# A two-layer decoder trunk: the first attention's beginning in written order, products issued ahead, contexts split as they end, and three smaller edits

## The chip, the cores and the metric

The kernel runs on one core of a Trainium2 chip. The metric is the device time of one execution in microseconds; the time before is the median of three runs. TensorE (PE) multiplies, VectorE (DVE), ScalarE (ACT) and GpSimd (POOL) work on tiles, and SyncE (SP) issues most transfers.

## The reference, cut to what matters

x is 512 tokens of 1024 features. Layer 0 mixes tokens with 16 heads of 64 whose scores carry a forgetting bias; layer 1 uses another attention that the change does not touch, apart from the order of its output projection.

```python
h = rms_norm(x, norm_mix_g[0])
proj = h @ fox_w_in[0]                      # q, k, v (1024 columns each) and 16 gate columns
cum = cumsum(log_sigmoid(gate + fox_b_f[0]), axis=tokens)
s = q @ k.T * 64**-0.5 + cum[query] - cum[key]      # causal
ctx = softmax(s) @ v
x = x + ctx @ fox_w_out[0]
x = x + square(relu(rms_norm(x, norm_ffn_g[0]) @ w_up)) @ w_down
...                                          # layer 1: latent attention, the same MLP
return rms_norm(x, final_norm_g)
```

## The kernel before, in words

Activations stand as tiles of 128 features by 512 tokens, so x is eight tiles and a linear layer is a sum over eight blocks of weights. Every number is split into a high part, rounded to the type that TensorE takes (ACT casts), and a low part, the rest (DVE subtracts). A product of two split numbers is three products: high by high, high by low, low by high (`three`, lines 260 to 269). One of 512 columns is what the texts call a product.

The root mean square is applied late: products are made of x times the gain, and the factor 1/rms of each token is multiplied into what comes out. It is computed from the sum of squares by token (`token_sums`, line 297, products with a column of ones), by three Newton steps (`rsqrt_of`, line 314, on GpSimd unless `alone`, then on DVE), and spread along a row by products with the identity (`along_tokens`, line 333; `rstd_tile`, line 341, copies it out).

Weights come in pieces of up to 128 x 1024, in the order of `pieces()` (line 74). `piece()` (line 250) hands out the next one and emits the load, cast and subtraction of it and of the one after. Two raw buffers and three of each part turn round (`raw`, `whi`, `wlo`).

The program is written as a sequence of tile operations. A scheduler then orders each engine's instructions by its own estimate of when operands are ready; where `order["on"]` names engines, their instructions stay in written order. Before the change this holds only in the MLPs and in the beginning of the second attention.

**The beginning (lines 470 to 559).** Eight x tiles, a gate piece of 128 columns and the first q and k pieces are loaded on SP's queue. Each x tile is scaled and split. Then PE makes the gate logits (24 products, the 16 gate columns padded to 128), q of the first head pair (24), the token sums, k (24) and the row of 1/rms. Then come four pieces of value weights, 24 products each, into four PSUM banks; after the first of these DVE finishes q and k (`qk_parts`) and the gate's running sum in nine doubling steps (`forget_sums`, line 522), which is stored to DRAM (`csc`) and loaded again, spread over partitions, as the bias tile `nb` of each pair (`start`, line 577).

**The attention (lines 415 to 449, 575 to 646).** A pair of heads takes four steps, of 512, 384, 256 and 128 keys. A step makes scores in two banks (`scores`), reduces, exponentiates and scales them on DVE and ACT (`soft_step`), and three steps later turns them by transposes (`turn_unit`). After a pair's last turn, `values` makes its context. Between steps a `Filler` issues products of coming work: 12 per step and 18 in the middle of a pair's end, `FILL1`, and 12 ahead of the first scores (line 643). Its work is, in order, q and k of pairs 1 to 7 (48 each), two groups of value columns (96 each) and parts of the output projection (`out_begin`, line 451) for three blocks and later two more. A part waits for its context (`ready`), and each context is split when the projection first asks for it (`ctx_part`, line 634). The other blocks of the projection follow in `out_proj` (line 648).

**The MLP (`ffn`, line 669)** runs by a list of due steps. In layer 0 `row` (line 756) makes the row of 1/rms; it is first used for the last eight blocks of hidden features (`up_post`, line 759).

**The end (`finish`, line 1299; `by_tokens`, line 1317).** The last eight output blocks of 128 tokens by 512 columns take 24 products each. After each the block is added to x, squared and summed, 1/rms is found by three Newton steps of two instructions, and two halves are scaled and stored.

## Time and profile before

| | us |
|---|---|
| median of three runs | 1130.95 (1130.09 to 1131.11) |
| the profiled execution | 1130.42 |
| its span, first to last instruction | 1128.6 |
| PE busy | 1113.4 |
| DVE busy | 781.4 |
| ACT busy | 581.3 |

The page gives busy time by engine and the chain that ended last. The timeline lists instructions in order of their start, repeated ones merged (xN); in square brackets stands how long the engine was idle before and what it waited for. A product's duration there includes its way through the array, so that products overlap: what one costs is read from the distance between starts. Nearly all operations are recorded through line 112, so tiles and stretches tell them apart: `acc`, `sc`, `tp`, `go`, `up`, `keep` are PSUM banks, `whi` and `wlo` parts of weights, `r` split activations, `t` temporaries.

### The profile page before, as it was taken

The numbers are of one execution on the slowest core, as the hardware profiler recorded it, in microseconds if no ns is written. First come the engines' busy times: TensorE is split into PE (matmuls) and PEld (weight loads), VectorE is DVE, ScalarE is ACT, GpSimd is POOL, SyncE is SP. The second block draws the span as 40 slices with busy tenths as digits, with TensorE's granted clock in tenths as the row PEclk, the third lists the DMA queues.
The fourth block names the chain that finished last, engine by engine and source line by source line (L and its number), as shares of the span: only waits on it lengthen the run. The fifth ranks groups of instructions, "written<-read, shape, count | busy, mean of one in ns | idle before, by whom it ended". The sixth has DMA issues, their size and how long they took to land.

```text
span 1128.6 us, 14263 instructions
## 1 busy us (share of the span) xinstructions
PE 1113.4 (99%) x5340; PEld 912.0 (81%) x5340; DVE 781.4 (69%) x1420; ACT 581.3 (52%) x1060; POOL 19.5 (2%) x71
## 2 busy tenths in 40 slices
PE   8999999999999999999999999999999999999997
PEld 6778887788888888888888877888888888888885
DVE  6797788764566667577895878738265765765784
ACT  5565665644555454434454767635465544444622
POOL 1000000001000000000001000000100000000000
PEclk9999999999999999999999999999999999999999
DMA  5422222143724415311344212213442611611402
GB/s 190 132 81 102 80 74 77 57 139 104 265 109 135 126 38 167 106 63 38 112 146 130 83 44 75 94 56 109 162 159 75 186 58 57 198 58 43 132 1 76
DMA packets 36822, 116.66 MB, mean 103 GB/s; under 512 B 4224, under 2 KB 4864, under 8 KB 36752
## 3 DMA queue, kind: packets, MB, share of 16 engines
q1 hardware_dynamic: 35888, 114.15, 31.1%
q10 hardware_dynamic: 864, 1.60, 0.4%
q8 instruction: 42, 0.69, 0.3%
q14 instruction: 28, 0.23, 0.1%
HBM read 109.40 MB, written 6.32 MB: 103 GB/s over the span
## 4 chain that ended last, share of the span: by engine, by line
PE 95%; DVE 2%; ACT 1%; DMA 1%; issue 0%; SPq 0%; ACTq 0%
PE up L112 35%; PE acc L112 20%; PE go L112 19%; PE sc L112 8%; PE tp L112 8%; PE keep L112 6%; DVE t L112 1%; ACT t L112 1%; DVE r L112 1%; DMA nb<-csc 0%; DMA t<-xT 0%; DVE wlo L112 0%; ACT whi L112 0%; ACT r L112 0%; DVE rs L112 0%
## 5 line engine op out<-in xcount | busy, mean ns | idle before, releaser
L112 PE MATMUL acc<-r,whi 128*128 128x512 f32 x606 | 196.4, 404 | 5.2 <-ACT whi L112 4.9
L112 PE MATMUL up<-r,r 128*128 128x512 f32 x808 | 192.7, 391 | 0.0
L112 PEld LDWEIGHTS up<-r,r 128*128 128x128 f32 x808 | 151.3, 188 | 31.4
L112 PE MATMUL up<-r,whi 128*128 128x512 f32 x544 | 170.9, 391 | 0.0
L112 DVE TENSOR_TENSOR wlo<-raw,whi 128x1024 fp32r<-128x1024 f32 (+3 forms) x95 | 111.4, 1173 | 48.3 <-ACT whi L112 37.6
L112 DVE TENSOR_TENSOR t<-s,t 128x512 fp32r<-128x512 f32 x84 | 58.0, 690 | 121.8 <-ACT t L112 121.7
L112 PEld LDWEIGHTS acc<-r,whi 128*128 128x128 f32 x606 | 111.1, 190 | 30.0 <-ACT whi L112 4.9
L112 ACT ACTIVATE s<-up 128x512 f32<-128x512 f32 x56 | 33.4, 597 | 190.0 <-PE up L112 190.0
L112 ACT CAST whi<-raw 128x1024 fp32r<-128x1024 f32 (+3 forms) x95 | 95.4, 1007 | 69.1 <-PE acc L112 30.6
L112 PE MATMUL acc<-r,wlo 128*128 128x512 f32 x303 | 119.7, 395 | 0.0
L112 PEld LDWEIGHTS up<-r,whi 128*128 128x128 f32 x544 | 101.8, 188 | 20.9
L112 PE MATMUL up<-r,wlo 128*128 128x512 f32 x288 | 112.3, 390 | 0.0
L112 PE MATMUL go<-r,t 128*128 128x512 f32 x360 | 86.5, 389 | 0.0
L112 PE MATMUL sc<-r,r 128*128 128x512 f32 (+7 forms) x480 | 80.0, 355 | 0.9 <-DVE sm L112 0.3
L112 PEld LDWEIGHTS go<-r,t 128*128 128x128 f32 x360 | 67.6, 188 | 14.0
L112 PE MATMUL go<-whi,t 128*128 128x512 f32 x240 | 78.8, 389 | 0.0
L112 PEld LDWEIGHTS sc<-r,r 64*128 64x128 f32 (+1 forms) x480 | 56.3, 186 | 23.6 <-issue 8.7
L112 PEld LDWEIGHTS acc<-r,wlo 128*128 128x128 f32 x303 | 57.5, 190 | 13.0 <-issue 0.4
L112 PEld LDWEIGHTS up<-r,wlo 128*128 128x128 f32 x288 | 54.1, 188 | 11.3
L112 DVE TENSOR_TENSOR r<-raw,r 128x512 fp32r<-128x512 f32 x72 | 47.3, 698 | 22.2 <-ACT r L112 22.1
L112 ACT ACTIVATE s<-s 128x512 f32<-128x512 f32 x64 | 40.5, 632 | 39.6 <-DVE s L112 37.8
L112 DVE TENSOR_TENSOR r<-q,r 128x512 fp32r<-128x512 f32 x94 | 60.5, 686 | 0.0
(199 smaller groups left out, 1863.7 us busy)
## 6 DMA issues: line engine op xcount, KB each, us to landing
raw<-wts SPq DMA_DIRECT2D x122, 512.0 KB, 3.6
q<-wts SPq DMA_DIRECT2D x56, 512.0 KB, 4.6
nb<-csc SPq DMA_DIRECT2D x8, 512.0 KB, 4.9
t<-xT SPq DMA_DIRECT2D x8, 256.0 KB, 5.9
r<-xT SPq DMA_DIRECT2D x8, 256.0 KB, 6.1
xmid<-r SPq DMA_DIRECT2D x8, 256.0 KB, 7.2
r<-xmid SPq DMA_DIRECT2D x8, 256.0 KB, 4.3
xkeep<-r SPq DMA_DIRECT2D x8, 256.0 KB, 2.2
```

The lines of the kernel that those rows point to most:

```text
L112: ins = fn(*args, **kw)
```

## The change

The beginning becomes one sequence in written order on PE, DVE, ACT and SP. The weights of q and k come in four quarters, each with the blocks of two x tiles. The first x tile, the gate weights and the second quarter are issued by ACT's queue, the gains and everything else by SP's. Nine products of a zero tile go ahead; then each x tile is scaled and used at once for two gate products (the high and low gate columns share one tile of 64 columns) and six of q and k. The sums of squares follow, token sums are made after the first value block of the first piece, the factor comes from DVE alone, and the row of 1/rms after the third block. The gate's work is spread between other DVE work, the value tiles become wider and fewer (twelve buffers become four of each of two kinds), and the filler issues 36 products ahead of the first scores instead of 12, then 11 and 18. Each context is split as its pair ends. The last block of an output projection takes another bank; the pieces ahead of the two output projections emit one piece more; the MLP's row in layer 0 goes through DRAM by GpSimd's queue; and the last output block is made in two halves of 256 columns, with one instruction less in the Newton steps. The diff, cut:

```diff
-FILL1 = (12, 18)
+FILL1 = (11, 18)
+IDLE = 9
-    out += [("qk", 1024)] * 2 + [("v", 1024)] * 4
+    out += [("qk0", 512)] * 4 + [("v", 1024)] * 4
+EARLIER = [[n for n, _ in PIECES].index(n) - 1 for n in ("fo", "mo")]
...
-        for j in (n, n + 1):
+        for j in range(n, n + 2 + (n in EARLIER)):
...
+    def row_by_dram(r):
+        line = keep.tile([S], F32, name=nm("line"))
+        nc.gpsimd.dma_start(line.rearrange("(b p) -> p b", p=P), r)
+        t = small.tile([P, S], F32, tag="rstd", name=nm("rstd"), bufs=2)
+        nc.gpsimd.dma_start(t, line.partition_broadcast(P))
+        return t
...
+        nc.scalar.dma_start(xs[0], xT[:, 0, :])
+        weights(nc.scalar, 0, fraw)
+        weights(nc.scalar, 2, raws[0][:, quarter[1]])
+        nc.scalar.copy(warm, ones)
+        nc.sync.dma_start(gsb, gains)
+        weights(nc.sync, 1, raws[0][:, quarter[0]])
+        for k in range(1, KD):
+            nc.sync.dma_start(xs[k], xT[:, k, :])
+            if k in (3, 5):
+                weights(nc.sync, (k + 3) // 2, raws[1][:, quarter[(k + 1) // 2]])
+        for _ in range(IDLE):
+            mm(fps, zero[:, :P], zero, start=True, stop=True)
+        def gate(k, j):
+            if j:
+                mm(fps[:32], fw[:, k, :32], h[k][1], start=False, stop=False)
+            else:
+                mm(fps[:64], fw[:, k], h[k][0], start=k == 0, stop=k == KD - 1)
         for k in range(KD):
+            j, c = k // 2, quarter[k // 2]
+            if k % 2 == 0 and k:
+                split(raws[j // 2][:, c], his[j // 2][:, c], los[j // 2][:, c])
+            h.append(scaled(xs[k], "mix0", k))
+            if k == 0:
+                nc.scalar.copy(fw[:, :, :FH], rv)
+                nc.vector.tensor_tensor(fw[:, :, 32 : 32 + FH], rv, f32(fw[:, :, :FH]), op=ALU.subtract)
+                split(raws[0][:, c], his[0][:, c], los[0][:, c])
+            for part in range(2):
+                gate(k, part if k < KD - 1 else 1 - part)
+            for n in range(2):
+                three(qk_ps[n], his[j // 2][:, b], los[j // 2][:, b], *h[k], k == 0, k == KD - 1)
+            if k == 5:
+                fetch(5)
...
+                if (kp, tb) == (0, 0):
+                    for b in range(NB):
+                        mm(ss[:, b : b + 1], acc[:, b * P : (b + 1) * P], ones, start=True, stop=True)
+                    for n in (6, 7):
+                        cast_piece(n)
+                        low_piece(n)
+                        fetch(n + 2)
+                    r = rsqrt_mean(ss, D, alone=True)
+                elif (kp, tb) == (0, 2):
+                    rstd = rstd_tile(r)
+                elif (kp, tb) == (0, 3):
+                    cast_piece(8)
+                    u, z, e = gate_logits()
...
+                    cur = running_sum(cur, (1, 2, 4, 8))
+                    qk[0].append(split(t))
+                    cast_piece(9)
+                    low_piece(9)
+                    cur = running_sum(cur, (16, 32, 64, 128, 256))
+                    nc.sync.dma_start(csc, cur)
...
-            whole[0] += e
+            if e:
+                split_ctx(p)
...
-            return out_begin("fo", tags, outs, lambda: whole[0], ctx_part)
+            return out_begin("fo", tags, outs, lambda: len(parts), lambda k: parts[k])
-        fill.run(12)
+        fill.run(36)
...
-                op = bank("acc")
+                op = bank("acc" if f < KD - 1 else "tp")
...
-                norm["row"] = rstd_tile(norm["rs"], "go")
+                norm["row"] = row_by_dram(norm["rs"])
...
+    def columns(tb, o):
+        return [slice(0, S)] if o or tb < NB - 1 else [slice(0, S // 2), slice(S // 2, S)]
+    def finish_squares(tb, n):
+        c = columns(tb, 0)[n]
+        nc.scalar.activation(out=tt()[:, c], in_=xtok[tb][0][:, c], func=AF.Square, accum_out=sums[:, 0, tb : tb + 1])
...
-        for m in (3.0, 12.0, 768.0):
-            nc.vector.scalar_tensor_tensor(out=a, in0=y, scalar=v, in1=y, op0=ALU.mult, op1=ALU.mult)
-            nc.vector.scalar_tensor_tensor(out=y, in0=a, scalar=-m, in1=y, op0=ALU.add, op1=ALU.mult)
+        nc.vector.scalar_tensor_tensor(out=a, in0=y, scalar=v, in1=y, op0=ALU.mult, op1=ALU.mult)
+        nc.vector.scalar_tensor_tensor(out=y, in0=a, scalar=-3.0, in1=y, op0=ALU.add, op1=ALU.mult)
+        nc.vector.scalar_tensor_tensor(out=a, in0=y, scalar=v, in1=y, op0=ALU.mult, op1=ALU.mult)
+        nc.vector.scalar_tensor_tensor(out=a, in0=a, scalar=-40.0 / 3, in1=a, op0=ALU.add, op1=ALU.mult)
+        nc.vector.scalar_tensor_tensor(out=y, in0=a, scalar=80.0, in1=y, op0=ALU.add, op1=ALU.mult)
...
+            dn[tb, o] = [bank(("up", "up", "go", "go", "up")[tb + n]) for n in range(len(columns(tb, o)))]
```

## Rows read from the trace of the kernel before

**Rows 1.** The page's busy times by engine: us, share of the span, instructions.

```profile
PE 1113.4 (99%) x5340; PEld 912.0 (81%) x5340; DVE 781.4 (69%) x1420; ACT 581.3 (52%) x1060; POOL 19.5 (2%) x71
```

**Rows 2.** The chain that ended last, in order of time: start us, us, what.

```profile
119.27 2.87 PE acc L112 x24
...
317.55 5.44 PE go L112 x24
...
1109.40 11.22 PE go L112 x48
```

**Rows 3.** Timeline of the first 32 us: start us, us, engine, line, operation.

```profile
1.05 0.91 DVE L112 MEMSET whi<- 128x1024 f32 x1 [0.19 <-issue]
...
3.91 0.72 ACT L112 ACTIVATE r<-t,gsb 128x512 fp32r<-128x512 f32 x1 [1.24 <-DMA gsb<-gains]
...
4.87 1.39 PE L112 MATMUL acc<-r,whi 128*128 128x512 f32 x2 [4.87 <-ACT whi L112]
...
6.12 0.72 ACT L112 ACTIVATE r<-t,gsb 128x512 fp32r<-128x512 f32 x1 [1.30 <-DMA t<-xT]
...
9.98 1.05 PE L112 MATMUL acc<-r,whi 128*128 128x512 f32 x2
...
10.83 0.47 PE L112 MATMUL acc<-r,wlo 128*128 128x512 f32 x1
...
20.19 0.95 PE L112 MATMUL tp<-ones,t 128*128 128x1 f32 x8
...
26.05 1.16 PE L112 MATMUL tp<-ident,rs 128*128 128x128 f32 x8
```

**Rows 4.** Windows by stage: busy time of each engine, granted clock, DMA.

```profile
49.00:202.00 153.00, 152.78 (x923) 124.20 (x921) 126.16 (x343) 91.22 (x218) 0.00 (x0) 1.00 0.28 90
202.00:222.00 20.00, 18.86 (x93) 13.59 (x93) 15.99 (x43) 10.84 (x28) 0.00 (x0) 1.00 0.18 54
```

**Rows 5.** Timeline of the last 10 us.

```profile
1120.65 0.75 DVE L112 SCALAR_TENSOR_TENSOR r<-go,r,r 128x512 f32<-128x512 f32 x1 [1.34 <-PE go L112]
1121.43 0.63 ACT L112 ACTIVATE t<-r 128x512 f32<-128x512 f32 x1 [2.15 <-DVE r L112]
...
1122.81 1.31 DVE L112 SCALAR_TENSOR_TENSOR fs<-fs,fs 128x1 f32<-128x1 f32 x6
```

**Rows 6.** Groups by shape in the first 52 us.

```profile
L112 DVE TENSOR_TENSOR wlo<-raw,whi 128x1024 fp32r<-128x1024 f32 x9 | 11.0, 1223 | 6.2 <-ACT whi L112 6.1
...
L112 ACT CAST whi<-raw 128x1024 fp32r<-128x1024 f32 x9 | 9.4, 1048 | 14.5 <-PE tp L112 7.3 <-PE acc L112 4.0 <-DMA raw<-wts 2.8
...
L112 DVE SCALAR_TENSOR_TENSOR v<-sc,rs,v 128x256 fp32r<-128x256 f32 x4 | 1.8, 480 | 1.1 <-ACT v L112 1.1
```

**Rows 7.** Timeline around 627 us, a reciprocal root on VectorE.

```profile
626.68 0.16 DVE L112 SCALAR_TENSOR_TENSOR rs<-sc,em 128x4 f32<-128x4 f32 x1 [0.19 <-PE sc L112]
...
628.66 0.36 DVE L112 SCALAR_TENSOR_TENSOR rs<-rs,rs 128x4 f32<-128x4 f32 x2
```

**Rows 8.** Timeline from 30 us, the gate sums' store and the first scores.

```profile
44.69 0.34 SPq L112 DMA_DIRECT2D csc<-t  x1
...
51.65 0.97 PE L112 MATMUL sc<-r,r 64*128 64x512 f32 x6
```

**Rows 9.** Timeline of the last pair of the first attention.

```profile
201.97 0.50 PE L112 MATMUL sc<-r,r 64*128 64x512 f32 x2
202.37 0.62 ACT L112 CAST r<-raw 128x512 fp32r<-128x512 f32 x1
...
205.30 0.44 PE L112 MATMUL tp<-ident,t 128*128 128x128 f32 x2 [0.90 <-DVE ptl L112]
...
205.76 0.69 DVE L112 CUSTOM_DVE_ANT_0 t<-sc,nb 128x512 f32<-128x512 f32 x1
```

**Rows 10.** Timeline of the first MLP's start.

```profile
283.82 1.05 PE L112 MATMUL go<-ident,rs 128*128 128x128 f32 x8
```

**Rows 11.** Instructions on the tile `rstd`: count, ns min/median/max, first and last start.

```profile
L112 DVE SCALAR_TENSOR_TENSOR s<-up,rstd x8: 691/692/696, 475.4 to 535.6; 128x512 f32<-128x512 f32 x8
```

More of the change, by code (lines that the diff above doesn't have):

```diff
@@ L179, in trunk @@
     warm = const.tile([P, 1], F32, name="warm")
-    nc.scalar.copy(warm, ones)
     maskz = const.tile([P, S], F32, name="maskz")
@@ L254, in piece @@
         state["next"] += 1
-        for j in (n, n + 1):
-            if j not in state["ready"] and j < len(PIECES) and not order["on"]:
+        for j in range(n, n + 2 + (n in EARLIER)):
+            if j not in state["ready"] and j < len(PIECES) and "vector" not in order["on"]:
                 emit_piece(j)
@@ L470, in trunk @@
         xs = [tt() for _ in range(KD)]
+        raws, his, los = (
+            [wpool.tile([P, 1024], dt, tag=t, name=nm(t), **kw) for _ in range(2)]
+            for t, dt, kw in (("raw", F32, {"bufs": 2}), ("whi", F32R, {}), ("wlo", F32R, {}))
+        )
+        zero = rt()
+        nc.vector.memset(f32(zero), 0.0)
+        fraw = f32(rt())[:, : KD * FH]
+        fw = wpool.tile([P, 1024], F32R, tag="whi", name=nm("whi"))[:, : KD * 64]
+        nc.vector.memset(f32(fw), 0.0)
+        fw = fw.rearrange("p (k c) -> p k c", c=64)
@@ new lines, in trunk, with weights @@
+        quarter = [slice(j % 2 * S, j % 2 * S + S) for j in range(4)]
+        def weights(queue, n, dst):
+            w = PIECES[n][1]
+            queue.dma_start(dst, wts[OFFS[n] : OFFS[n] + P * w].rearrange("(p w) -> p w", p=P))
+        nc.scalar.dma_start(xs[0], xT[:, 0, :])
[4 more added lines that the diff above has]
+        weights(nc.sync, 1, raws[0][:, quarter[0]])
@@ L485, in trunk @@
-        qk = {}
-        qk_ps = []
-        for _ in range(2):
-            qk_ps.append(bank("acc"))
-            linear(qk_ps[-1], piece("qk"), h)
-            if len(qk_ps) == 1:
-                r = rstd_of(acc, D)
-        rstd = rstd_tile(r)
+            if k == 2:
+                cast_piece(5)
+                low_piece(5)
+                fetch(6)
+                fetch(7)
+            square_sum(acc, xs[k], k == 0, xs[k])
         def qk_parts(pp, scale):
@@ L537, in forget_sums, with running_sum @@
+        def running_sum(cur, ds):
+            for d in ds:
                 nxt = tt()[:FH]
@@ L561, in v4_gen @@
+        vts = [value_high((0, 1), tb, accs[tb]) for tb in range(NB)]
+        for tb in range(NB):
+            value_low((0, 1), tb, accs[tb], vts[tb])
+            if tb == 1:
+                cast_piece(10)
+                low_piece(10)
+                fetch(12)
+        order["on"] = ("tensor",)
+        for e in ("vector", "scalar"):
+            order["last"].pop(e)
         def v4_gen(q):
@@ L595, in scores @@
                     mm(scs[e][:, :n], a[rows, q], b2[rows, :n], start=st, stop=sp)
+            order["on"] = ()
+            order["last"].clear()
             nb = nbs[p]
@@ L1335, in block_mm, with block_add @@
         def block_mm(tb, o):
-            dn[tb, o] = bank(("up", "up", "go", "go")[tb])
             t = slice(tb * P, (tb + 1) * P)
-            for i in range(4):
-                for j in range(2):
-                    k = i // 2 * 4 + j * 2 + i % 2
-                    three(dn[tb, o], *los["w", o, i][j], sh[k][:, t], sl[k][:, t], i == 0 and j == 0, i == 3 and j == 1, flip=True)
+            dn[tb, o] = [bank(("up", "up", "go", "go", "up")[tb + n]) for n in range(len(columns(tb, o)))]
+            for c, dst in zip(columns(tb, o), dn[tb, o]):
+                for i in range(4):
+                    for j in range(2):
+                        k = i // 2 * 4 + j * 2 + i % 2
+                        w = [p[:, c] for p in los["w", o, i][j]]
+                        three(dst[:, c], *w, sh[k][:, t], sl[k][:, t], i == 0 and j == 0, i == 3 and j == 1, flip=True)
+        def block_add(tb, o, n):
+            c = columns(tb, o)[n]
+            xt = xtok[tb][o][:, c]
+            nc.vector.scalar_tensor_tensor(out=xt, in0=dn[tb, o][n][:, c], scalar=fn["norm"]["r2"][:, tb : tb + 1], in1=xt, op0=ALU.mult, op1=ALU.add)
         for k in range(KD):
@@ L1386, in _pack @@
     parts.append(_cols(fw, 3 * W, FH))
-    parts += [_cols(fw, 0, P), _cols(fw, W, P)]
+    first = [_cols(fw, 0, P), _cols(fw, W, P)]
+    parts += [np.concatenate([b[:, 2 * j : 2 * j + 2] for b in first], axis=1) for j in range(4)]
     b = _cols(fw, 2 * W, S)
```

129 lines of the change are left out of this document (63 added, 66 removed).

## The prediction, before the result was known

> **What bounds the kernel now.** I read the page's busy times first: TensorE (PE) is busy for all but 15 us of the span [rows 1], so time can only come from fewer or faster products, or from places where PE waits. The chain of waits gives the pace: 24 products of 512 columns take 5.44 us, 0.227 us each; 24 of 256 columns take 2.87 us, 0.12 us each [rows 2]. That pace holds through both MLPs and most of the rest. The timeline of the start comes next: PE's only large wait is the 4.87 us before its first product, and from there to 10.83 us the products start 0.43 us apart, the pace of 512 columns at 1.2 GHz; then it doubles, after products had run for 6 us [rows 3]. The windows by stage show the last: from 202 to 222 us PE is idle for 1.1 us, while VectorE (DVE) is busy for 16.0 of 20 us [rows 4]. The final stretch is a chain of DVE and ScalarE (ACT) work behind the last product [rows 5].
>
> **The start.** Before, 24 gate products and 48 of q and k, with the 0.95 us of token sums between them, end at 26.05 us; without the sums that is 25.1 [rows 3]. After, there are 16 gate products (the 16 gate columns and their low parts share one product) and the same 48: 64 x 0.227 = 14.5 us at full pace, 8 x 0.227 = 1.8 less. Ahead of them nine products of zeros run as soon as a 512-column memset is done; half of the 0.91 us of the 1024-column one from 1.05 [rows 3] puts that at 1.5 us. At 0.43 each they end at 5.3.
>
> The first gate product needs x0's high part (0.72 us on ACT) and the gate's weights, whose low part is queued on DVE behind x0's low part, 0.75 us as for any such pass of 512 columns [rows 5]. Before, x0's scaling began at 3.91 [rows 3]; now x0 and the first q/k quarter (256 KB) come on two queues at once. I take x0 at 4.2 and the first product at 6.05. When does the pace double? Before, 6.0 us after the first product; the zeros move that to 7.5, if they count as work. Bounds: at 5.3, as the zeros end, or 6 us after the first real product, 12.0. x1 was scaled from 6.12, 2.2 us after x0, with 64 KB between them [rows 3]. Now two q/k quarters of 256 KB stand before it or beside it; at up to that 2.2 us for 256 KB it could be 4 us late, but the queues carry both together, so I estimate 2 us: 8.0, and after 0.72 and 0.75 us its low part at 9.5. Then 55 products at 0.227 remain: the end is at 22.0, or 21.3 if x1 does not bind. I take **21.7, a gain of 3.4 us**. Bounds: 20.6 (clock doubled at 5.3, x1 as before: 6.05 + 14.5; gain 4.5) and 23.3 (clock at 12.0: 14 products at 0.43, 50 at 0.227; gain 1.8). ACT and DVE have 8 scalings, 4 quarter splits and the gate's own each, some 9 us in 15: covered.
>
> **The wait for the row of 1/rms.** Before, GpSimd (POOL) computes it beside the second q/k block, from the sums at 20.19 to the row products at 26.05 [rows 3], and PE hardly waits. After, all its steps are DVE's, written behind the low parts of two weight pieces. The first of those pieces needs the buffer that the last q/k product frees. So on DVE: 0.25 + 1.05 (cast) + 2 x 1.23 + 2.35 (the same twelve steps took from 626.68 to 629.02) = 6.1 us after the q/k end [rows 6, 7]. PE reaches the row products after three blocks of six and the sums: 18 x 0.227 + 0.95 = 5.0. **Loss 1.1 us**; bounds 0 and 1.3. Behind the row product on PE stand the fourth block and everything after it. So the value block ends 2.3 us earlier than before. SP's queue now passes the quarters before the late x tiles; that is in x1's term. The scans of the gate sums end on DVE 15 us of work after the row, some 2 us before the value block does, about when they did before (their store is issued at 44.69, scores start at 51.65) [rows 8]. The first scores now come 36 products later, not 12, which covers the 7 us from that store to the first use of the loaded biases; without the 24 the scores would wait for them some 3 us. That cover costs nothing here: the 24 products (5.4 us) were due anyway.
>
> **The end of the first attention.** Before, when the output projection's parts begin, ACT and DVE get a burst from 202.37 us on: a weight piece split in halves, then all six contexts so far, each a cast of about 0.62 and a subtraction of about 0.69 us. PE waits 0.9 us for the subtraction of a transposed tile queued among them [rows 9]. From 201.97 to 205.5 PE does six score products, 0.97 us at the first pair [rows 8], and eight transposes of 128 columns at 0.11, the pace of [rows 10]: 1.9 us of work in 3.5. After, the contexts are split as their pairs end, and one weight piece is emitted before the parts begin. That moves 0.69 us of DVE to each pair's 23 us, in a stage where DVE has 27 of 153 us free [rows 4]: free. The burst loses 6 x 0.69 + 1.23 = 5.4 us of DVE, though the halves stay. **Gain 1.7 us**, bounds 0 and 2.5 (the stretch after it is ragged too). But the 24 products issued ahead are missing later. Counting the calls of the filler: steps 28, 29, 30 had 12, 12, 6 products, and now have 6, 0, 0, since the projection's parts wait for the seventh context. There PE has only scores and transposes, and the scores wait for DVE to free two banks. DVE's work in steps 28 to 31 (two reductions at 0.69 us for the longest [rows 9], mask, scaling, two subtractions: an estimate of 4 us for the longest step, 1.5 for the shortest) is some 12 us, PE's some 10.8. **Loss 1.2 us**, bounds 0 and 5.4 (all 24 products' time as waits). The pair is -0.5.
>
> The value tiles shrink from twelve to four of a wider kind plus four: the last group of values reuses the first ones' and waits until pair 3 is done. Its blocks fill three banks by then, and PE has scores to do; zero, up to 1 us.
>
> **The MLP's row by DRAM.** Eight products of 1.05 us leave PE [rows 10]; the next product would have started 0.9 us earlier. The replacement is two POOL transfers of 512 numbers; the row is first used 190 us later [rows 11], so even a slow transfer is covered. **Gain 0.9 us.** No queue of POOL is used before, and what one costs at the launch no row shows; bounds 0 and +1, taken as 0, since its engine already has its share of the prologue.
>
> **The tail.** The last block comes in two halves of 256 columns, 48 x 0.12 = 5.76 us against 24 x 0.234 = 5.61 [rows 2]: +0.15. Behind it, the addition falls from 0.75 to the 0.48 of a 256-column one [rows 5, 6], the square by an estimated 0.2 of its 0.63, and one of six steps of 0.22 goes: -0.7. **Gain 0.55 us.** The first half's addition and square lie beside the second half's 2.9 us.
>
> **Costed at nothing.** The projection's last block in a "tp" bank (no wait stands there now; cover is the preceding block's 5.4 us), and weight pieces emitted one earlier ahead of both projections (DVE and ACT have room).
>
> **Sum:** -3.4 + 1.1 - 0.5 - 0.9 - 0.55 = -4.25 us. The profiled execution took 1130.42 us, its span 1128.6; the median of the runs is 1130.95, 0.5 more. From the median: **1126.7 us**.
>
> **Rivals.** (a) x0 lands late. The timeline of before has one queue carrying nearly everything, and x1, third on it, is worked on 2.2 us after x0 [rows 3]. If the ACT queue's x0 has to share with SP's quarter to the end, x0 lands where x1 did: first product 8.0, q/k end 22.5 to 23.3. That costs 1.2 us: 1127.9. For it: transfers of equal size on two queues; against it: x0 is issued first. The Trainium skill's "DMA: Bandwidth & Descriptors", section "Queues, rings and completion order", says that each engine alternates packet by packet between the queues, which speaks for it; no run here shows it yet. Chance 0.20.
> (b) Everything goes well: early clock, no wait for the row, the burst's full 2.5 us back and no lack of products: -4.5 + 0 - 2.5 - 0.9 - 0.55 = -8.45, or 1122.5. For it: DVE is free enough; against it: the row's chain is written behind two low parts. Chance 0.17.
> (c) The zeros do not bring the clock forward (gain at the start 1.8 less 1.1) and the lack of products costs 3 us against the burst's 1.7: -0.7 + 1.3 - 1.45, or 1130.1. Chance 0.15.
> (d) Slower: steps 28 to 31 run at DVE's pace, with every one of the 24 products missed (+5.4, the burst not recovered), and the start at its lower bound with the full row wait (-0.5): +3.4, or 1134.4. It decides once DVE's chain through the two score banks takes over 5 us more than PE's own work there. For it: DVE at 80% there even with 24 more products on PE; against it: 5.4 us of the burst leave DVE. Chance 0.08.
> That the change does not do what it says is hard to see: the products taken out are in the code.
>
> **The numbers.** The forecast has 0.40. Differences under 0.2% (2.26 us) can't be told from none by this measurement. Faster: forecast, (a) and (b), 0.77; within: (c), 0.15; slower: (d), 0.08. The range runs from case (b) to (c), and a little past it for the unknown cost of POOL's queue: 1122.5 to 1130.7.
>
> **What would show it.** Nine products before 5.5 us, a 0.227 pace from about 7.5, the first row product near 28 with a wait of about 1 us, PE idle in the last pair's steps but no burst of casts, no products from the identity in the MLP, and under 7.4 us from the last product to the span's end. Wrong it would be if the pace doubles only near 12 us, if PE idles over 4 us in the last pair, or if the scores wait for the biases.

## The result: 0.2% slower

The changed kernel takes 1133.0 us (median of 10 runs, 1132.1 to 1135.1) against 1130.4 for the kernel before (10 runs): a ratio of 1.0021, with a 95% interval of 1.0013 to 1.0030. The prediction was 1126.7, "faster". The profiled execution of the changed kernel took 1132.99 us with a span of 1131.2, 2.6 over before's 1128.6, and the landmarks below divide these 2.6 us. Each is the start time on PE, in us from the span's start; a step is one block of scores of the first attention.

| landmark | before | after | difference |
|---|---|---|---|
| first value product (q and k done) | 26.96 | 21.98 | -4.98 |
| scores of step 0 | 51.65 | 53.88 | +2.23 |
| scores of step 2 | 59.15 | 64.90 | +5.75 |
| scores of step 27 | 196.55 | 202.39 | +5.84 |
| first MLP product | 261.11 | 263.36 | +2.25 |
| first closing product of the first MLP (the first into a `keep` bank) | 339.15 | 340.47 | +1.32 |
| first scores of the second attention | 653.47 | 655.56 | +2.09 |
| first product of the second MLP | 782.56 | 785.85 | +3.29 |
| last product | 1120.21 | 1123.32 | +3.11 |
| end of the span | 1128.60 | 1131.22 | +2.62 |

The gain of the start is there, but the first row overstates it: before, the token sums and the row of 1/rms stand ahead of that product, after the change behind it. Counted to the end of the first 24 value products (32.52 and 29.30) it is 3.2 us. The gain is lost by step 2, more than half of that loss is won back at the end of the attention, and then time is lost again behind the first closing product, in stretches that the change hardly touches.

The page's busy line of the changed kernel, which answers to [rows 1]:

```profile
PE 1117.2 (99%) x5357; PEld 913.2 (81%) x5357; DVE 781.1 (69%) x1424; ACT 581.2 (51%) x1060; POOL 17.6 (2%) x61
```

PE has 17 products more than before and is busy 3.8 us longer; DVE and ACT did what they did before, and POOL is busy 1.9 us less.

The start of the changed kernel in the timeline (start, us, engine, line, operation, tiles, shape, and in brackets the idle time ahead and what ended it), which answers to [rows 3]:

```profile
1.49 4.21 PE L114 MATMUL acc<-r 128*128 128x512 f32 x9 [1.49 <-DVE r L114]
...
4.03 0.72 ACT L114 ACTIVATE r<-t,gsb 128x512 fp32r<-128x512 f32 x1 [0.39 <-DMA t<-xT]
...
5.79 1.45 PE L114 MATMUL acc<-r,whi 128*64 128x512 f32 x4
...
7.31 0.62 PE L114 MATMUL acc<-r,whi 128*128 128x512 f32 x2
...
7.64 0.72 ACT L114 ACTIVATE r<-t,gsb 128x512 fp32r<-128x512 f32 x1 [1.77 <-DMA t<-xT]
...
21.90 2.37 DVE L114 TENSOR_TENSOR wlo<-raw,whi 128x1024 fp32r<-128x1024 f32 x2 [0.41 <-ACT whi L114]
21.98 0.39 PE L114 MATMUL sc<-whi,r 128*128 128x512 f32 x1
...
24.33 0.16 DVE L114 TENSOR_SCALAR rs<-tp 128x4 f32<-128x4 f32 x1
...
26.31 0.36 DVE L114 SCALAR_TENSOR_TENSOR rs<-rs,rs 128x4 f32<-128x4 f32 x2
...
27.02 1.05 PE L114 MATMUL tp<-ident,rs 128*128 128x128 f32 x8
```

The nine products of zeros run from 1.49 us, x0 is scaled at 4.03, the gate's first product follows at 5.79, and at 7.31 two products take 0.62 us, the pace of the upper clock. (Seven of the runs below have the same beginning; in their profiled executions q and k are done at 20.73 to 21.91 us, so up to 1.25 us of any difference between two of these executions lies in the start.) The root of the mean is done on DVE at 26.67, ahead of the row products at 27.02, which have no wait in front of them.

The first steps of the attention in the timeline of the changed kernel, all engines (this stretch holds the loss that the prediction had not seen):

```profile
47.83 0.34 SPq L114 DMA_DIRECT2D csc<-t  x1
...
49.05 1.20 DVE L114 TENSOR_TENSOR wlo<-raw,whi 128x1024 fp32r<-128x1024 f32 x1
...
49.42 0.34 SPq L114 DMA_DIRECT2D nb<-csc  x1
...
50.27 0.33 SPq L114 DMA_DIRECT2D raw<-wts  x1
...
50.66 0.42 SPq L114 DMA_DIRECT2D nb<-csc  x1
...
53.56 0.43 DVE L114 TENSOR_TENSOR nb<-nb,maskz 128x256 f32<-128x256 f32 x1 [0.26 <-DMA nb<-csc]
...
53.88 0.97 PE L114 MATMUL sc<-r,r 64*128 64x512 f32 x6
...
56.05 1.05 ACT L114 CAST whi<-raw 128x1024 fp32r<-128x1024 f32 x1 [2.09 <-DMA raw<-wts]
...
57.13 1.22 DVE L114 TENSOR_TENSOR wlo<-raw,whi 128x1024 fp32r<-128x1024 f32 x1 [2.45 <-ACT whi L114]
58.28 0.68 DVE L114 CUSTOM_DVE_ANT_0 t<-sc,nb 128x512 f32<-128x512 f32 x1
...
59.02 0.44 PE L114 MATMUL sc<-r,r 64*128 64x384 f32 x1 [1.22 <-DVE sm L114]
...
61.17 1.06 PE L114 MATMUL acc<-r,whi 128*128 128x512 f32 x2
...
64.90 0.62 PE L114 MATMUL sc<-r,r 64*128 64x256 f32 x6
```

The biases land by 53.56, before the first scores end at 54.8, so the first reduction (CUSTOM on DVE) could start when these end. It starts at 58.28. Ahead of it in DVE's order stands the low part of a weight piece, which waits 2.45 us for a cast that waits for a load. The load was issued only at 50.27, because the buffer it needs was read until then (the low part of 49.05 to 50.25), and it took 5.67 us to land, with the loads of the first biases ahead of and behind it on the same queue. The chain that ended last has it as one piece:

```profile
50.27 5.67 DMA raw<-wts
```

The second scores wait for DVE, which must first read the banks that they go into. Then the products at 61.17 take 1.06 us a pair instead of 0.62: the clock has fallen. The windows show it (columns as in [rows 4]: length, busy time of PE, PEld, DVE, ACT and POOL with counts, granted clock, DMA share, GB/s):

```profile
49.00:61.10 12.10, 10.71 (x49) 7.73 (x48) 9.08 (x17) 5.06 (x8) 0.00 (x0) 1.00 0.62 214
61.10:64.50 3.40, 3.40 (x9) 2.69 (x9) 3.40 (x9) 2.17 (x6) 0.00 (x0) 0.50 0.05 18
64.50:70.00 5.50, 5.50 (x35) 4.11 (x34) 4.52 (x15) 2.78 (x8) 0.00 (x0) 1.00 0.29 95
```

For 3.4 us PE runs at 1.2 GHz, half of its upper clock, which costs some 1.7 us; ahead of it stands a stretch with 1.4 us of idle time. In the kernel before, PE is not idle from 49.0 to 61.1 us, and the clock does not fall there.

The end of the attention in PE's timeline, where [rows 9] showed a wait of 0.90 us behind the burst:

```profile
212.63 0.50 PE L114 MATMUL sc<-r,r 64*128 64x512 f32 x2
...
213.72 0.50 PE L114 MATMUL sc<-r,r 64*128 64x512 f32 x1
...
215.28 0.72 PE L114 MATMUL sc<-r,r 64*128 64x512 f32 x3
...
220.05 0.33 PE L114 MATMUL tp<-ident,t 128*128 128x128 f32 x1 [0.56 <-DVE ptl L114]
```

The burst is gone, but the six score products of one step, 0.97 us where nothing holds them, are strewn over 3.3 us, with seven products between, and transposes still wait for DVE.

The tail in the timeline, which answers to [rows 5]:

```profile
1123.64 0.48 DVE L114 SCALAR_TENSOR_TENSOR r<-up,r,r 128x256 f32<-128x256 f32 x1 [0.45 <-PE up L114]
1124.20 0.42 ACT L114 ACTIVATE t<-r 128x256 f32<-128x256 f32 x1 [1.27 <-issue]
...
1126.27 0.16 DVE L114 SCALAR_TENSOR_TENSOR fs<-fs,fs 128x1 f32<-128x1 f32 x1
```

Addition and square are 0.27 and 0.21 us shorter, and from the start of the last product to the span's end it is 7.90 us instead of 8.39.

### The profile page after: what moved, and what is told of

The parts are those of the page before. It is cut to its first block, busy times and chain, and to the rows that moved or that the text cites. A ratio compares the mean times of both kernels' runs of the same rounds, so it can differ in the third digit from the quotient of the medians.

```text
span 1131.2 us, 14303 instructions
## 1 busy us (share of the span) xinstructions
PE 1117.2 (99%) x5357; PEld 913.2 (81%) x5357; DVE 781.1 (69%) x1424; ACT 581.2 (51%) x1060; POOL 17.6 (2%) x61
## 4 chain that ended last, share of the span: by engine, by line
PE 92%; DVE 4%; ACT 2%; DMA 1%; issue 1%; SPq 0%; ACTq 0%
PE up L114 35%; PE go L114 18%; PE acc L114 18%; PE tp L114 8%; PE sc L114 7%; PE keep L114 6%; DVE t L114 2%; ACT t L114 1%; DVE wlo L114 1%; DMA t<-xT 1%; DMA raw<-wts 1%; DVE r L114 0%; DMA nb<-csc 0%; ACT whi L114 0%; ACT r L114 0%
## 5 line engine op out<-in xcount | busy, mean ns | idle before, releaser
L114 PE MATMUL up<-r,r 128*128 128x512 f32 (+1 forms) x820 | 194.6, 388 | 0.0
L114 PE MATMUL acc<-r,whi 128*128 128x512 f32 (+1 forms) x574 | 185.1, 405 | 0.8 <-DVE r L114 0.3
L114 PEld LDWEIGHTS acc<-r,whi 128*128 128x128 f32 (+1 forms) x574 | 103.8, 188 | 26.0 <-ACT r L114 1.7
L114 PE MATMUL acc<-r,wlo 128*128 128x512 f32 x279 | 110.1, 394 | 0.0
L114 PEld LDWEIGHTS acc<-r,wlo 128*128 128x128 f32 x279 | 52.8, 189 | 12.2
L114 DVE TENSOR_TENSOR wlo<-q,whi 128x1024 fp32r<-128x1024 f32 x45 | 54.9, 1220 | 7.9 <-ACT whi L114 7.5
```

Of the source, the lines that this page charges most:

```text
L114: ins = fn(*args, **kw)
```

## The experiments

All are the changed kernel or the kernel before with the one edit shown. Where only one run was taken, its landmarks are all there is, and they carry the spread of the start given above. A ratio is to the kernel before, measured along with the run.

**e1: 24 products ahead of the first scores instead of 36.**

```diff
-        fill.run(36)
+        fill.run(24)
```

> 24 products ahead of the first scores instead of 36, all else as changed. Theory (queue on VectorE): in the changed kernel the first score reduction (58.28 us) stands on VectorE behind the low part of a weight piece that only the products 25 to 36 ask for, and that piece's load lands late; PE then waits 1.9 us in all and its clock falls for 3.4 us. With 24 the piece is asked for after the first scores: first scores near 51.2, reductions by 54, second scores by 56 (now 59.0), no fall of the clock near 61, and 12 products more left for the last pair. Time 1129 to 1130 (3 to 4 us under the changed kernel). Rival (bias load): the biases land at 53.5 whatever is issued, so 12 fewer products ahead leave PE waiting as long, 1 to 2.7 us, and the clock falls as before: 1132 to 1134. Rival (too few products at the end): the first scores do not matter, only the 12 products that return to the last pair: the gain stands after 200 us and is 1 to 2 us.

Measured: 1129.7 us (ratio to before 0.9992, interval 0.9983 to 1.0002), 3.3 under the changed kernel. The first reduction starts at 54.55, right behind the biases, but the third scores then wait 1.09 us for DVE, which waits for a weight piece's cast, and the clock falls at 62.7, which the theory had excluded. Of the 2.79 us by which step 0 starts earlier, 2.30 are still there at the span's end: twelve products fewer ahead (2.72 us at 0.227) make nearly their whole time.

**e2: two unused small tiles, so that all later pools lie 64 bytes higher, as before the change.** The change drops one tag of 2 x 32 bytes from the small pool.

```diff
+    pad = [small.tile([P, 1], F32, tag="fs2", name=nm("fs"), bufs=2) for _ in range(2)]
+    for t in pad:
+        nc.gpsimd.memset(t, 0.0)
```

> Two unused one-column tiles bring the small pool back to its size, so that every buffer pool after it lies at the addresses of the kernel before (64 bytes higher than in the changed kernel); nothing else changes. Theory (address): PE's pace where it reads from those pools follows the address: the second output projection goes back from 0.2345 to 0.2267 us a product (755 to 786 us: -1.1 us), the eight blocks that close the first MLP from 0.2315 to 0.229 (-0.4), and the last eight blocks from 0.2311 back to 0.2333 (+0.4): -1.0 us in sum, all of it after 550 us. Rival (the other bank, the earlier pieces): pace unchanged, within 0.2 us. The start and the first attention stay as in the changed kernel.

Measured: 1131.1 us (1.0002, interval 0.9992 to 1.0011). From the first MLP's closing blocks to the second attention 314.34 us, after 315.09, before 314.32; the second output projection 46.72, after 47.77, before 46.74. With the second attention itself and the last blocks some 1.6 us come back behind the first MLP's middle. So the pace follows the addresses, more than the theory's 1.0 us. The profiled execution had no fall of the clock at 61 us either, and a span of 1126.9: there the late weight piece's load is issued at 50.00 and its cast starts at 54.64, instead of 50.27 and 56.05, and step 2 starts 8.28 us behind step 0, against 11.02 in the changed kernel and 7.50 before. So up to 2.7 us of the loss in the first steps differ from one execution to the next, with the same order of work. The median counts for the whole time, 1.9 us under the changed kernel.

**e3: contexts split when the projection first uses them, as before, with 36 products ahead.**

```diff
-            if e:
-                split_ctx(p)
+            whole[0] += e
```

(with the old `ctx_part` in `out_gen`).

> Contexts are split again only when the projection's parts ask for them, all else as changed. Theory (too few products): the last pair of the first attention in the changed kernel loses time because steps 28 to 30 have 6, 0, 0 products left, not because of the contexts: undoing the split gives a burst of six casts and subtractions in which PE loses 1 to 2 us more, so the first MLP starts 1 to 2 us later than 263.4. Rival (spreading costs): the extra 0.69 us of VectorE per pair delays the steady steps; undone, the steps from 65 to 190 us are earlier by up to 1 us and the MLP starts earlier.

Measured: 1138.3 us in one run, 5.3 over the changed kernel, where the theory had 1 to 2. The MLP starts later, not earlier, which is against the rival. The burst of splits now stands ahead of the reductions of the steps before the last pair: PE waits 2.14 us ahead of the scores at 200.07, and the clock is at half for 6.8 us twice, from 198.6 and from 225.9.

**e4: 12 products ahead, and the filler's numbers as before.**

```diff
-FILL1 = (11, 18)
+FILL1 = (12, 18)
...
-        fill.run(36)
+        fill.run(12)
```

> 12 products ahead and 12 and 18 in the steps, as before the change, all else as changed. Theory (queue on VectorE): first scores near 48.4, but VectorE has the gate sums' scans, the values' low parts and two weight pieces until about 53 and the biases land at 53.5, so the reductions start near 54 and PE, with 12 products to do, waits some 3 us before its second scores near 55.5; the clock falls. Against the changed kernel the start loses about as much as it loses now, and the last pair gets all its products back: the MLP starts 1 to 3 us earlier than 263.4. Rival (bias load alone sets the first reduction): second scores at 55, no clock fall, MLP at 259 to 260.

Measured: 1127.7 us in one run, 3.1 under before, 5.3 under the changed kernel. The scores of step 1 wait (they start at 53.73, before the change at 55.49, although step 0 starts 4.35 us earlier than there), since the biases land at 52.40; there is no fall of the clock, and the MLP starts at 258.0. That is the rival's picture, and not the theory's. The end of the attention tells what the 24 products are worth. The windows from the scores of step 27 to the first MLP product, here and then in the changed kernel (columns as above):

```profile
196.24:258.00 61.76, 61.75 (x317) 50.12 (x317) 44.74 (x98) 33.22 (x71) 0.00 (x0) 1.00 0.32 102
```

```profile
202.39:263.36 60.97, 59.28 (x294) 46.91 (x293) 41.94 (x98) 31.56 (x69) 0.00 (x0) 1.00 0.30 95
```

With 24 products fewer the stretch is only 0.79 us shorter. The second row counts 1.7 us of idle PE. The rest of the loss it counts as busy, since a product's duration covers its way through the array: in the timeline the starts of scores, transposes and the values' products lie some 0.1 to 0.8 us further apart than their pace.

**e5 and e11: 12 and 18 products ahead, with the addresses of before.** e4's edit and e2's; e11 with `fill.run(18)`.

> The changed kernel with only 12 products ahead of the first scores (and the filler's 12, 18 as before) and with the two unused 4-byte tiles that put every later pool 64 bytes higher again. Theory (the 24 extra products ahead cost some 5 us where scores, DVE and the last pair run without cover, and the addresses cost 1.4 us): the two corrections add up, 1127.7 less 1.4 = 1126.3 us, 4.4 under the kernel before, ratio 0.996; second output projection at 0.227 us a product, no fall of the clock in 60 to 66 us. Rival (the one look at 12 products ahead was a lucky run, or the two corrections overlap): 1127.5 to 1128.5 us.

> The kernel of run e5 with 18 products ahead of the first scores instead of 12. Theory (12 products leave the second scores waiting 1.2 us for biases that come late, and each product put ahead costs up to its own time in the last pair): the second scores wait under 0.5 us, some 0.7 us more are lost at the end, 1126.0 to 1126.9, no difference that can be told from 12. Rival (with 18 the loss starts as with 24 and 36, the clock falls at 62 us): 1127.5 to 1129.

Measured: e5 1126.6 us (0.9965, interval 0.9950 to 0.9979), as the two corrections add up. It is 4.3 us under the kernel before (1126.57 against 1130.89), e2 is 0.3 over it (1131.09 against 1130.76). The two differ only in the 24 products and in 12 for 11 in `FILL1`, so repeated runs price these at some 4.6 us, the first steps included. e11 1125.0 us (0.9950, interval 0.9936 to 0.9963), faster than both kernels, though neither of its texts came true: the second scores still wait 1.54 us, the clock falls at 56.6 for 3.4 us, and by step 2 it is 1.9 us behind e5; by step 27 it is level again, and it ends first; what brings it level is open. The intervals of the two overlap, so which is the better one is not settled; both are under the kernel before.

**e6: the kernel before, with its later pools 64 bytes lower.**

```diff
-        v, a, y = (small.tile([P, 1], F32, tag=f"fs{j}", name=nm("fs"), bufs=2) for j in range(3))
+        v, a, y = (small.tile([P, 1], F32, tag=f"fs{min(j, 1)}", name=nm("fs"), bufs=2) for j in range(3))
```

> The kernel before, unchanged but for one thing: the tail's three 4-byte vectors share two tags instead of three, so that the small pool is 64 bytes smaller and every pool opened after it lies 64 bytes lower, as in the changed kernel. Theory (the addresses alone set the pace of the second half's products): second output projection 0.2345 us a product instead of 0.2267, the blocks that close the first MLP 0.2315 instead of 0.229, the last blocks of the second MLP a little faster; in sum +1.0 to +1.6 us: 1131.8 to 1132.4. Rival (the slower pace belongs to another part of the change: the other bank for the projection's last block, the weight piece that is emitted earlier, the rows by DRAM): the paces and the time of before, 1130.4 to 1130.9.

Measured: 1132.5 us (1.0012, interval 1.0003 to 1.0021), the span 1.57 longer. The chain at the second output projection (start, us, what), before and then in this kernel, whose instructions stand in the same order:

```profile
766.41 16.32 PE acc L112 x72
```

```profile
767.82 16.88 PE acc L112 x72
```

72 products take 16.88 us instead of 16.32: 0.2344 us each instead of 0.2267. In the changed kernel it is 11.25 for 48, the same 0.2344:

```profile
769.14 11.25 PE acc L114 x48
```

Besides the addresses, e6 differs only in which of the small tiles share a buffer in the last blocks, far behind this stretch. So the addresses alone make this pace. (The traces hold no addresses: the 64 bytes are the room of the dropped tag in the program.)

**e7: no products of zeros.**

```diff
-IDLE = 9
+IDLE = 0
```

> The changed kernel without the nine products of zeros ahead of the gate's. Theory (the zeros are what brings the doubling of the pace forward, and they cost nothing since x0 isn't there before 5.8 us): first product at 5.8 to 6.1 us, 0.43 us a product up to 11 or 12 us, q and k end at 23.3 to 24.0 instead of 21.98, the whole time 1.4 to 2.0 us over the changed kernel. Rival (the clock rises by itself, whatever ran before): the pace doubles at 6.5 to 7.5 us, q and k end at 22.0, the time is the changed kernel's.

Measured: 1134.7 us in one run, 1.7 over the changed kernel's profiled run. Its timeline:

```profile
6.13 1.97 PE L114 MATMUL acc<-r,whi 128*64 128x512 f32 x4 [6.13 <-DVE whi L114]
...
9.60 1.91 PE L114 MATMUL acc<-r,whi 128*64 128x512 f32 x4
...
12.38 1.08 PE L114 MATMUL acc<-r,whi 128*64 128x512 f32 x4
```

Four products take 1.9 us until 11.6 and 1.08 from then on, and q and k end at 23.36. That is 1.4 us later than in the changed kernel's profiled execution, and 1.4 to 2.6 later than in all eight with the zeros. The zeros are worth that.

**e8: the low part that stood in the way goes behind the first two reductions.** An order-only dependency on DVE; `reduced` holds the reductions of `soft_step` as they are written.

```diff
-        nc.vector.tensor_tensor(lo, fetched.pop(n)[:, :w], f32(hi), op=ALU.subtract)
+        ins = nc.vector.tensor_tensor(lo, fetched.pop(n)[:, :w], f32(hi), op=ALU.subtract)
+        if n == 12:
+            tc.add_manual_dep(ins.ins, reduced[1].ins.name, mybir.DependencyInfo(mybir.DependencyClass.NoSync, mybir.DependencyReason.DATA), reason="as written")
```

> The changed kernel with one weight piece's low part (the one at 57.13 us, 1.22 us on DVE) put behind the first two score reductions in DVE's order instead of ahead of them; nothing else moves. Theory (the scores of steps 0 and 1 were late because DVE stood 2.45 us at that low part, whose weights landed late): the first reduction at 54.7 us instead of 58.28, the second scores at 55.5 to 56.0 instead of 59.02, the wait ahead of them under 0.2 us; by the third scores 1 to 3.5 us of it are left, 1129.5 to 1132 in all, with or without the fall of the clock at 61 us. Rival (the biases, which landed at 53.5, or the scores themselves set the first soft step): first reduction later than 56 us, second scores at 58 to 59.

Measured: 1131.3 us in one run. Its timeline of the same stretch:

```profile
54.09 0.68 DVE L114 CUSTOM_DVE_ANT_0 t<-sc,nb 128x512 f32<-128x512 f32 x1
...
56.87 1.23 DVE L114 TENSOR_TENSOR wlo<-raw,whi 128x1024 fp32r<-128x1024 f32 x1 [1.48 <-ACT whi L114]
59.70 0.17 DVE L114 RECIPROCAL sm<-sm 128x2 f32<-128x2 f32 x1 [1.61 <-ACT t L114]
...
62.11 1.09 PE L114 MATMUL sc<-r,r 64*128 64x256 f32 x6 [1.46 <-DVE sm L114]
```

The reduction starts at 54.09 instead of 58.28, the second scores at 56.90 without a wait. So the low part was in the way, as the theory had it, though it put these scores at 55.5 to 56.0. Some 0.8 us of the 4.2 are an earlier start of this execution (first scores at 53.04 instead of 53.88). But the wait moves to the third scores (62.11), since ACT casts the late piece and loads a table (1.28 us) before the exponentials. Here the clock does not fall. By step 2 the run is 2.8 us ahead, by the span's end 1.7, these 0.8 included.

**e9: the kernel before with its contexts split as each pair ends.** The edit of e3, reversed, on the kernel before.

> The kernel before with one part of the change: each context of the first attention is split as its pair ends, not when the output projection's parts first use it. Theory (from the accounting of the runs with 12 products ahead, which have the end of the attention 2.8 us shorter): from the first scores of the last but one pair's last step (196.55 before) to the first MLP product (261.11) 61.5 to 62.2 us instead of 64.56, in all 1127.7 to 1128.7. Rival (the gain comes from the weight piece that the change emits one earlier there, which this kernel does not do): under 1 us of gain, 1129.7 or more.

Measured: 1128.1 us (0.9977, interval 0.9968 to 0.9986). From the scores of step 27 to the first MLP product 61.73 us instead of 64.56: the part alone is worth 2.83 us.

**e10: the kernel before with the MLP's row of 1/rms by POOL transfers.**

```diff
-                norm["row"] = rstd_tile(norm["rs"], "go")
+                norm["row"] = row_by_dram(norm["rs"])
```

> The kernel before with the MLPs' row of 1/rms by two POOL transfers instead of products. Theory: from the first MLP product to the first closing product 77.1 us instead of 78.04, nothing else changes, 0.9 us under the kernel before; the second MLP likewise has no row, so nothing there. Rival (a queue of POOL's own costs at the launch or at the span's end): less than 0.4 us gained or a loss, with the first instruction or the end later.

Measured: 1129.7 us in one run. From the first MLP product to the first closing one 77.11 us instead of 78.04: 0.93 gained, no loss at the launch or the end.

**e12: the kernel before with 36 products ahead of the first scores.**

```diff
-        fill.run(12)
+        fill.run(36)
```

> The kernel before with 36 products instead of 12 ahead of the first scores, and nothing else. Theory (products put ahead are missing in the last pair, where scores, DVE and transposes then run without cover; case (d) of the prediction): first scores at 57.0 instead of 51.65, of these 5.4 us at most 1.5 are given back by 261 us, in all 3.5 to 5.0 us slower, 1134 to 1136. Rival (the prediction's own sum: the products are due anyway and only some of their time is lost): 0.5 to 1.5 us slower, 1131 to 1132.

Measured: 1138.0 us (1.0065, interval 1.0051 to 1.0079), 7.2 slower, more than either text said. Steps 0 to 2 follow each other as before (3.84 and 3.66 us), 5.4 later: the products ahead do not disturb them. But the burst of splits now begins at 198.5, a step earlier than before, and lies on DVE among the reductions that free the banks of steps 26 and 27. Its PE timeline, and its windows behind that:

```profile
200.68 0.55 PE L112 MATMUL sc<-r,r 64*128 64x128 f32 x3 [2.15 <-DVE sm L112]
...
218.45 0.97 PE L112 MATMUL sc<-r,r 64*128 64x512 f32 x6
```

```profile
201.50:204.90 3.40, 3.40 (x9) 2.32 (x8) 2.90 (x12) 0.78 (x3) 0.00 (x0) 0.50 0.81 273
204.90:225.40 20.50, 19.57 (x103) 14.95 (x101) 11.75 (x31) 9.95 (x26) 0.00 (x0) 1.00 0.01 3
225.40:232.20 6.80, 6.80 (x28) 5.94 (x28) 5.31 (x22) 3.47 (x12) 0.00 (x0) 0.50 0.00 0
```

After waits of 1.0 and 2.15 us the clock is at half for 3.4 us, and again for 6.8 from 225.4; half of both is 5.1 us. What the 24 products would cost in this kernel without these falls is not shown.

## Why the prediction was wrong

By the prediction's own terms, from the landmarks and single runs (most rows are differences of landmarks, so that they nearly add up proves nothing; what carries them is the runs named):

| term | predicted | measured |
|---|---|---|
| start, and the row of 1/rms behind it | -3.4 + 1.1 | -3.2 (no wait for the row) |
| contexts spread (the burst) | -1.7 | -2.8 (e9) |
| 24 products that are missing later | +1.2 | +4.65 (5.44 ahead, 0.79 given back: e4) |
| first steps of the attention | 0 | +3.5 (in e2's execution +0.8) |
| MLP row | -0.9 | -0.93 (e10) |
| tail | -0.7 + 0.15 | -0.49, the +0.15 in the row below |
| addresses | not named | +1.8 (e6: +1.6) |
| sum | -4.25 | +2.5 of the +2.62 |

**The start** went as predicted: nine products from 1.49, the upper clock by 7.3, q and k done at 21.98 (20.73 to 21.91 in the seven other executions) against 21.7. x1 was scaled at 7.64, predicted 8.0. Without the zeros (e7) the clock rises only at 11.6, close to the prediction's lower bound of 6 us after the first real product. Rival (a), x0 sharing its way to the end, did not come: x0 was scaled at 4.03, only 0.1 later than in [rows 3]. The Trainium skill's "DMA: Bandwidth & Descriptors", section "Queues, rings and completion order", has each engine alternate between queues by packets. The trace does not contradict it, since x1, behind more bytes, is 1.5 us later than before; it can't show how far x0 shared, since the scaling of before waited for the gains.

**The wait for the row** (+1.1) did not come. The prediction had DVE begin with a cast after the last q and k product, 6.1 us until the root is done. The cast began at 20.81, before that product, and the two low parts at 21.90; the root was done 4.7 us after q and k, and the first row product came at 27.02 without idle time. Here its lower bound of 0 was right.

**The burst** gave 2.8 us (e9), more than the prediction's upper bound of 2.5. Its 1.7 was read from 201.97 to 205.5 us alone; how the 2.8 spread over the stretch behind is not shown.

**The 24 products** are, with the first steps, the step that failed most, by 3.45 us. "That cover costs nothing here: the 24 products (5.4 us) were due anyway" holds only if PE can use the time that they leave at the end. It can't: steps 28 to 31 have scores that wait for banks and DVE work, and 24 products fewer shorten the stretch by 0.79 us (e4 against the changed kernel). The prediction had set DVE's 12 us against PE's 10.8 and taken the difference. That is a balance of totals; the gaps between the short dependent pieces are no part of it. Its upper bound of 5.4 (all 24 lost), which stood in rival (d), was nearly reached. That rival, 1134.4 in all, came nearest to the 1133.0, but in part by luck: it had the burst not recovered, which gave 2.8 us, and a start at its lower bound with the full wait for the row, which did not come. The first steps and the addresses, which it did not have, made up for both.

**The first steps** (+3.5) had no term. The prediction had the start of the first scores rightly (54.8 by its terms, 53.88 measured), and the biases land in time for them, but two things on DVE were wrong or missing. It counted 15 us of DVE work from the row of 1/rms to the end of the gate's scans, which put that end 2 us before the value block's and the store where it was, at 44.69. In the trace the store is issued at 47.83, 2.2 us behind the end of the value block (the first filler product starts at 45.62):

```profile
33.82 1.28 ACT L114 ACT_TABLE_LOAD   x1
...
35.75 0.60 ACT L114 CAST r<-t 128x512 fp32r<-128x512 f32 x1
...
36.38 0.69 DVE L114 TENSOR_TENSOR r<-t,r 128x512 fp32r<-128x512 f32 x1 [3.97 <-ACT r L114]
...
45.62 0.61 PE L114 MATMUL acc<-r,whi 128*128 128x512 f32 x2
```

```profile
26.67:47.83 21.16, 21.16 (x99) 17.66 (x98) 13.61 (x29) 11.44 (x16) 0.00 (x0) 1.00 0.19 68
```

From the root at 26.67 it takes 21.2 us, of which DVE works 13.6; the rest are waits, the longest of 3.97 us behind ACT's gate functions, a table load and a cast. Again a sum of work stood for a chain. No run moves the scans alone, so what this costs is not shown.

It also did not ask what stands ahead of the first reduction on DVE. The new order leaves behind the scans four value passes and two low parts (47.73 to 52.7), so a raw buffer comes free late, at 50.25. The load into it lands 5.67 us later, and the low part of that piece blocks the reduction behind it. That the bias loads beside it make this load slow is likely, but no run shows it. e8 shows the block: reordered, the reduction starts 4.2 us earlier and the second scores have no wait. e12 shows that the products ahead alone are not the cause: with 36 of them and the old beginning, steps 0 to 2 take what they took (7.50 us from step 0 to step 2). With the new beginning they take 10.3, 11.3, 10.3 and 11.0 in the profiled executions with 12, 18, 24 and 36 products (e4, e11, e1 and the changed kernel); with 12 and 18 it is the biases that land late, at 52.40 and 53.11. Of the 3.5 us some 1.7 are the clock at half; e8, without the fall, still loses 1.6 in steps 0 to 2, and e2's execution 0.8. The fall and the late load are not the same in every execution: of the ten of the changed kernel, the two with the highest mean granted clock (0.999) took 1132.1 us, the two with the lowest (0.995) 1134.8 and 1135.1; the profiled one, at 0.996, stands at the median.

**The addresses** (+1.8) are a part of the change that the prediction missed: its tail merges two small tiles, and everything allocated behind the small pool moves by 64 bytes. e6 does this alone to the kernel before and gets the slower pace. The prediction took the pace of each stretch as it stood before, 0.227 us and in the last blocks 0.234, and did not ask what sets it; in the second output projection it is 0.2267 or 0.2344, by the addresses. The Trainium skill's "TensorE: Matmul & The Clock Gate", section "Wait — 56ns, not 53.3ns?", gives 215.7 ns for it at the upper clock, columns over clock plus a fixed 2.5 ns. No run here shows that: the fastest 24 products in a row, before and after, take 226.6 ns each. And no address enters it; the measurement decides.

**The MLP's row** was right within 0.1 us. **The tail** gave 0.49 us behind the last product, where 0.7 was counted: up to the last scaling the chain is 0.8 us shorter (3.14 instead of 3.95), but from there to the span's end it takes 4.76 instead of 4.44, for a reason that is open. The other bank for the projection's last block and the value tiles' reuse left no wait in the trace; they were not tried alone.

Of what the prediction said would show it wrong ("if PE idles over 4 us in the last pair, or if the scores wait for the biases") neither happened as put: the stretch counts 1.7 us of idle PE, the rest of the loss lies in gaps between starts, and the scores waited for DVE. Of what it said would show it, the wait of 1 us for the row did not come, and from the last product to the span's end it is 7.6 us even from that product's end, not under 7.4.

What stays open: what the late scans cost by themselves; why the clock falls behind a wait of 1.1 to 1.5 us in some executions (the changed kernel, e1, e11) and not behind one of the same size in others (1.20 us in e4, 1.46 in e8); why the cast behind the same load starts 4.6, 5.8 or 6.4 us after its issue (e2, the changed kernel, e8); and which operand's address it is that slows the products.

## What to carry to other kernels

Work that fills waits is worth what it covers, at both ends: before moving products to the front, look at what will run beside them where they are missing, and price them there by the gaps of the dependent chain (here 4.65 us) and not by the balance of two engines' totals (1.2). Where a stage's start depends on a short chain on DVE, list what stands ahead of it in that engine's order and when the inputs of each of these land, buffers and loads included. And compare addresses before and after: a tile dropped from a small pool moved everything behind it, and that alone was worth 0.1% (e6).

## What was not expected of the hardware

- The pace of products of 512 columns depends on where operands lie in SBUF: 64 bytes lower, 0.2344 instead of 0.2267 us in the second output projection (e6), while the last blocks of the second MLP get a little faster (from its first product into a `keep` bank to the last product 256.3 us instead of 256.7).
- The two transfers on POOL's queue, a row of 2 KB to DRAM and that row back to all partitions, took 10.4 and 7.1 us from issue to landing (8.9 and 6.6 in e10). Both of the changed kernel's, in POOL's timeline; the second waits for the first:

```profile
274.65 0.95 POOL L341 DMA_DIRECT2D line<-rs  x1
285.37 0.57 POOL L343 DMA_DIRECT2D rstd<-line  x1 [9.77 <-DMA line<-rs]
```

  The row is first used at 476.7, over 180 us later.
- Short waits were dear twice: behind 1.4 us of idle time in the changed kernel, and behind waits of 1.0 and 2.15 us in e12, the clock fell to 1.2 GHz (for 3.4 us, and for 10.2 in all), and each of these microseconds costs half of one while PE is busy.
